# The last expert's second down group without split weights, other PSUM banks for some transposes, and a padded tile: a hybrid decoder trunk on one core

## The chip, the cores and the metric

One core of a Trainium2 chip runs the whole program in one launch. The metric is the device time of that launch in microseconds (us), lower is better. A measurement is the median over several runs; the profile is of one run more.

## The reference

Two layers on 512 tokens of width 1024, all in float32. Each layer is `h = LN(ALPHA*h + mixer(h))`, then `h = LN(ALPHA*h + FFN(h))`. The mixer is one projection `h @ w_in`, sparse attention and a short convolution, and an output projection by `w_o`. The FFN of layer 0 is a dense SwiGLU; that of layer 1, which ends the program, is a mixture of eight experts of hidden width 1408, of which each token takes two:

```python
for e in range(N_EXPERTS):
    out = out + gate[..., e:e + 1] * swiglu(h, wg[e], wu[e], wd[e])

def swiglu(h, wg, wu, wd):
    return (jax.nn.silu(h @ wg) * (h @ wu)) @ wd
```

The final layer norm follows, and its 512x1024 result is the output.

## The kernel before

**Products of split numbers.** A float32 operand is split into a high and a low part, and a product is three TensorE matmuls: high by high, low by high, high by low (`mm3`, L198). In the mixer and the dense FFN the parts are of type float32r (`split`, L141); in the expert stage they are float16. There `split16_ops` (L869) makes the high part on ScalarE (L873) and the low part on VectorE (L874), after a scaling by 256.

**The expert stage** (`moe`, L1005). The experts are sorted by load and taken in the order of `TURN`. Expert number e has a fixed room for tokens, `CAPS[e]`: 160, 168, 152, 144, 136, 132, 128, 128. The six with more than 128 rows deliver their result in two pieces of rows (`chunks`, L33). The hidden width is worked in two groups of 6 and 5 blocks of 128 (`groups`, L1010). For each expert and group the kernel streams pieces of the gate weight, the up weight and the down weight: `eblock` (L848) loads a piece by SyncE's queue into one of nine buffers, `split16` splits it, TensorE multiplies. `expert_gate` (L903) applies Silu; `expert_hidden` (L909) multiplies by the up product on VectorE (L913), then rounds to float16 on ScalarE (L914) and takes the rest on VectorE (L915), which gives the two parts `hh` and `hl`.

For the two experts with 128 rows the down product is by rows: the hidden parts are the stationary operand and the weights move through in two halves of 512 columns (`expert_down_rows`, L932, matmuls at L947). For the other six it is transposed, and `expert_out` (L979) turns it back: per piece of rows and half of the columns four TensorE transposes (L986) fill a PSUM bank, and ScalarE scales them out (L987). PSUM has eight banks by tag (L50): "mm" 2, "tr" 2, "s" 3, "po" 1. In `expert_out` the first half uses an "mm" bank and the second the only "po" bank, for both pieces. The code of `expert_out` is called behind the first piece of the next expert's first up product. The "s" banks hold the down product of an expert; they were emptied by `expert_end` (L967) just before.

**The end.** Once the last expert's gate product of group 0 is issued, GpSimd's queue fetches the sum over the other experts: 512 rows into `h` (L1064), and the rows that the last expert will change into `xl` (L1065). With the second group of the last expert all comes together. VectorE takes the statistics of the four tiles of `h` (`row_stats`, L993, and L1083); `roots` (L1021) gives one over the deviation (Sqrt on ScalarE, two small operations on VectorE); `rows_scaled` (L999) is two passes of 128x1024 per tile on VectorE, and `store` (L990) writes the tile by SyncE's queue. `last_rows` (L1040) adds a half of the last expert's product to `xl` (L1042) and takes its statistics (L1043). After both halves VectorE normalises `xl`, and GpSimd scatters its rows over the stored ones (L1114).

The order of instructions on each engine is laid down by a planner, which goes by program order among what is ready. `issue_after(x)` keeps VectorE's instructions of a block behind x. `self.low` is the latest split's VectorE instruction. So the statistics wait for the last up weight's split, and the scaling of the four tiles for the last down weight's split.

**The output projection of layer 1** (`out_proj`, L566). A pool holds the split pieces of W_o: seven of eight pairs of 128x1024 in it, the first in the common ring. In layer 1 three small tiles of the router lie ahead of them in the same pool (`route_sums`, L652): 512, 512 and 64 bytes per partition. In layer 0 nothing lies ahead of them.

Of the kernel before, what the change touches and what calls it, by code (L numbers as in the profile page):

```python
# [7 lines left out]
F32 = mybir.dt.float32  # L8
# [5 lines left out]
OP = mybir.AluOpType  # L14
# [3 lines left out]
S, D, NT, KD = 512, 1024, 4, 8  # L18
# [5 lines left out]
NE, FE, NFE = 8, 1408, 11  # L24
# [8 lines left out]
def chunks(e):  # L33

    c = CAPS[e]
    return [(0, c)] if c <= 128 else [(0, CH), (CH, c - CH)]


def by_rows(e):

    return CAPS[e] == 128


def packed(n, e):

    k = 512 // CAPS[e]
    return [(i, min(k, n - i)) for i in range(0, n, k)]
# [3 lines left out]
XS, WS, HS, GS = 2.0 ** 6, 2.0 ** 8, 2.0 ** 5, 2.0 ** 12  # L51
# [3 lines left out]
class Trunk:  # L55
# [596 lines left out]
    def route_sums(self, tp):  # L652


        nc = self.nc
        ones = tp.tile([128, 128], F32, name="ones32")
        nc.gpsimd.memset(ones, 1.0)
        x = tp.tile([128, 2, NE, KD], F32, name="gw")
        own = self.wr.rearrange("p k e -> p e k")
        for i in range(2):  # L660
            nc.vector.tensor_tensor(x[:, i], own, self.factors[:, i][:, None, :].to_broadcast([128, NE, KD]), op=OP.mult)
        nc.vector.tensor_copy(own, x[:, 0])
        s = tp.tile([128, 2, NE], F32, name="gs")
        nc.vector.tensor_reduce(s, x, axis=AX.X, op=OP.add)
        p = self.psum("po")
        nc.tensor.matmul(p[:, 0:2 * NE], ones, s.rearrange("p i e -> p (i e)"), start=True, stop=True)
        nc.vector.tensor_scalar(self.wsum[:, 0], p[:, 0:NE], -1.0, None, op0=OP.mult)
        nc.vector.tensor_copy(self.wsum[:, 1], p[:, NE:2 * NE])
# [234 lines left out]
    def expert_gate(self, parts):  # L903
# [2 lines left out]
            self.nc.scalar.activation(g[:, c], x, AF.Silu, scale=1.0 / (XS * WS))  # L906
        return g

    def expert_hidden(self, parts, g):  # L909
        nc = self.nc  # L910
        hh, hl = (self.mp.tile([128, 6 * CAP], F16, name=x, bufs=2) for x in ("ehh", "ehl"))
        for x, c in parts:
            nc.vector.scalar_tensor_tensor(g[:, c], x, HS / (XS * WS), g[:, c], op0=OP.mult, op1=OP.mult)  # L913
            nc.scalar.activation(hh[:, c], g[:, c], AF.Copy)  # L914
            nc.vector.tensor_tensor(hl[:, c], g[:, c], hh[:, c], op=OP.subtract)  # L915
        return hh, hl
# [12 lines left out]
                             lambda k: (hi[:, k - k0, c], lo[:, k - k0, c], hh[:, r(k)], hl[:, r(k)]), k0, k1,  # L929
                             first=f0 + k0 == 0 and m == 0, last=f0 + k1 == NFE and m == nm - 1, shared=True)  # L930

    def expert_down_rows(self, i0, e, f0, n, hh, hl, ys, finish=None):  # L932

        held = []
        for k0 in range(0, n, 2):
            k1 = min(n, k0 + 2)
            src = self.weights("moe_wd", i0, e, slice((f0 + k0) * 128, (f0 + k1) * 128), slice(0, D))
            hi, lo = self.split16(self.eblock([128, k1 - k0, D], src))
            held += [(k0 + k, hi[:, k], lo[:, k]) for k in range(k1 - k0)]
            if finish is not None and 0 < k0 and k1 < n:  # L940
                continue
            for half, y in enumerate(ys):
                c = slice(half * 512, half * 512 + 512)
                for k, h, l in held:
                    r = slice(k * 128, k * 128 + 128)
                    for a, b in ((hh, h), (hl, h), (hh, l)):
                        self.nc.tensor.matmul(y, a[:, r], b[:, c], start=f0 + k == 0 and a is hh and b is h,  # L947
                                              stop=f0 + k == NFE - 1 and b is l)
                if finish is not None and k1 == n:
                    finish(half)  # L950
            held = []

    def expert_rows(self, e, ys):

# [24 lines left out]
    def expert_out(self, e, yt):  # L979
        nc = self.nc  # L980
        for r, (s, n) in enumerate(chunks(e)):
            yr = self.mp.tile([128, D], F32, name="yr", bufs=2)[0:n]
            for half in range(2):
                p = self.psum("po" if half else "mm")
                for k in range(4):
                    nc.tensor.transpose(p[0:n, k * 128:(k + 1) * 128], yt[:, half * 4 + k, s:s + n], self.ident)  # L986
                nc.scalar.activation(yr[:, half * 512:half * 512 + 512], p[0:n], AF.Copy, scale=self.sgate[0:n, e, r:r + 1])  # L987
            self.add_rows(e, r, yr)
# [16 lines left out]
    def moe(self, l):  # L1005
        nc = self.nc
        mp = self.mp = self.pool("moe%d" % l)
        i0 = l // 2
        self.nblock = 0
        groups = [(0, 6), (6, 5)]  # L1010
# [10 lines left out]
        def roots(rs, mv):  # L1021
            nc.scalar.activation(rs, mv[:, :, 1:2], AF.Sqrt, bias=self.eps[0:rs.shape[0]], scale=ALPHA ** 2)
            nc.vector.reciprocal(rs, rs)
            nc.vector.tensor_scalar(rs, rs, ALPHA, None, op0=OP.mult)
# [8 lines left out]
        gb = end[:, 0:2]  # L1033
        self.ln_load(gb, self.t["ln2_g"][l], self.t["ln2_b"][l])
        final = TURN[-1]
        xl = end[:, 2]
        mv = mp.tile([128, NT, 2], F32, name="mv4")
        st2 = self.small.tile([128, 2, 6], F32, name="st")

        def last_rows(half, y):  # L1040
            c = slice(half * 512, half * 512 + 512)
            nc.vector.scalar_tensor_tensor(xl[:, c], y, self.sgate[:, final, 0:1], xl[:, c], op0=OP.mult, op1=OP.add)  # L1042
            nc.vector.bn_stats(st2[:, half], xl[:, c])  # L1043

        def ended(e, hid, ys):
            if by_rows(e):
                self.expert_down_rows(i0, e, *groups[1], *hid, ys)
                self.expert_rows(e, ys)
                return None
            self.expert_down(i0, e, *groups[1], *hid, ys)  # L1050
            return self.expert_end(e, ys)
        before = None
        for turn, e in enumerate(TURN):
            last = e == final
            after = None if last else TURN[turn + 1]
            xg = None if last else self.gather(after)
            up = lambda name, g, **kw: self.expert_up(i0, e, name, *groups[g], xs, **kw)

            gate = self.expert_gate(up("moe_wg", 0))
            yt = before and ended(*before)  # L1060
            if last:

                for tt in range(NT):
                    nc.gpsimd.dma_start(self.h[:, tt], self.abuf[tt * 128:(tt + 1) * 128])  # L1064
                nc.gpsimd.indirect_dma_start(out=xl, out_offset=None, in_=self.abuf[:, :],  # L1065
                                             in_offset=bass.IndirectOffsetOnAxis(ap=self.idx[:, e, 0:1], axis=0))
            out = (lambda: self.expert_out(before[0], yt)) if yt is not None else None
            hid = self.expert_hidden(up("moe_wu", 0, mid=out), gate)
            if turn + 2 < NE:
                self.slot_data(TURN[turn + 2])  # L1070
            gate = self.expert_gate(up("moe_wg", 1))
            ys = [self.psum("s") for _ in (range(2) if by_rows(e) else packed(KD, e))]
            (self.expert_down_rows if by_rows(e) else self.expert_down)(i0, e, *groups[0], *hid, ys)
            if turn == 0:
                self.slot_data(e)
            nxt = []
            mid = None if last else (lambda: nxt.extend(self.gather_t(after, xg)))
            hid = self.expert_hidden(up("moe_wu", 1, mid=mid), gate)
            before, xs = (e, hid, ys), nxt

        with self.tc.issue_after(self.low.ins):
            for tt in range(NT):
                nc.vector.bn_aggr(mv[:, tt], self.row_stats(self.h[:, tt]))  # L1083
            rs = self.small.tile([128, NT, 1], F32, name="rs4")
            roots(rs, mv)
            nc.vector.tensor_tensor(self.bad[:, 0:NT], mv[:, :, 1], mv[:, :, 1], op=OP.not_equal)

        def finish(half):
            if half == 0:
                with self.tc.issue_after(self.low.ins):  # L1090
                    for tt in range(NT):
                        self.rows_scaled(self.h[:, tt], mv[:, tt, 0:1], rs[:, tt], gb)
                        self.store(tt)
            last_rows(half, ys[half])
        self.expert_down_rows(i0, final, *groups[1], *hid, ys, finish)

        nl, nh, xl = 128, 1, end[:, 2:3]
        mv2 = mp.tile([nl, nh, 2], F32, name="mv2")
# [8 lines left out]
        p = self.psum("tr")  # L1107
# [3 lines left out]
        for r in range(nh):  # L1111
            self.rows_scaled(xl[:, r], mv2[:, r, 0:1], rs2[:, r], gb)
            i = self.dst[0:nl, final, r:r + 1]
# [121 lines left out]
```

## Time and profile before

| | |
|---|---|
| median of 3 runs (lowest to highest) | 1373.26 us (1372.77 to 1375.89) |
| the profiled run, its own time | 1373.08 us |
| span of its trace | 1371.2 us |
| mean granted TensorE clock | 0.994 of full speed |
| TensorE matmuls busy | 1329.4 us, 97% |
| VectorE busy | 867.5 us, 63% |
| ScalarE busy | 667.7 us, 49% |

The times in rows are microseconds from the start of the span. A matmul's duration is modelled from entering the array to leaving it, so neighbours overlap, and the pace of a row of matmuls is the distance of their starts. PEld is TensorE's load of the stationary operand. A busy share over the whole span says little here, since the engine that limits is another one at the end than before it; the views are read by stage.

### The profile page before, as it was taken

The page shows a single profiled execution, that of the slowest core. Times are in us where ns is not written, and L with a number is a line of the kernel's source. Part 1 is how long each engine was busy: PE and PEld are TensorE (multiplying, and loading weights), DVE is VectorE, ACT ScalarE, POOL GpSimd, SP SyncE. Part 2 cuts the span into 40 slices and gives each one's busy share as a digit, 9 for nine tenths or more (in the row PEclk, how much of TensorE's full clock was granted, in tenths as well). Part 3 has the DMA queues.
Part 4 walks back from the last instruction along what each step waited for, and adds up shares of the span by engine and source line. Part 5 has one row for each costly group of instructions (what it writes and reads, how often), then busy time and mean ns, then how long its engine had stood idle before and what let it go on. Part 6 is the DMA issues. An engine that isn't in the chain of part 4 may idle for free.

```text
span 1371.2 us, 26845 instructions
## 1 busy us (share of the span) xinstructions
PE 1329.4 (97%) x11478; PEld 1155.6 (84%) x11478; DVE 867.5 (63%) x1260; ACT 667.7 (49%) x948; POOL 72.4 (5%) x86
## 2 busy tenths in 40 slices
PE   5999999999999999999999999999999999999993
PEld 5888788898888888888887888889999999999872
DVE  7567665743333332228556665769688787788897
ACT  3575443323222322213565553427677677687881
POOL 3000000000000000000000000010011011010130
PEclk9999999999999999999999999999999999999997
DMA  8442020332323222322562020659899899899992
GB/s 254 128 123 62 32 62 33 122 102 83 123 66 118 92 95 104 109 92 60 158 165 63 31 63 1 218 218 364 299 350 355 275 345 372 308 353 370 384 377 103
DMA packets 137887, 241.10 MB, mean 176 GB/s; under 512 B 12891, under 2 KB 82619, under 8 KB 137765
## 3 DMA queue, kind: packets, MB, share of 16 engines
q1 hardware_dynamic: 132948, 223.20, 47.9%
q0 software_dynamic: 4816, 16.17, 4.1%
q8 instruction: 90, 1.47, 0.4%
q14 instruction: 33, 0.26, 0.1%
HBM read 227.75 MB, written 11.68 MB: 175 GB/s over the span
## 4 chain that ended last, share of the span: by engine, by line
PE 90%; DVE 6%; ACT 2%; issue 1%; DMA 1%; SPq 0%; POOL 0%; POOLq 0%; DVEq 0%; ACTq 0%
PE mm L205 47%; PE s L205 16%; PE tr L205 10%; PE po L491 3%; PE s L509 2%; PE s L475 2%; DVE wlo L874 1%; PE s L383 1%; PE po L205 1%; PE tr L475 1%; PE tr L509 1%; PE s L947 1%; DVE h L1002 1%; DVE h L1003 1%; PE tr L190 1%
## 5 line engine op out<-in xcount | busy, mean ns | idle before, releaser
L205 PEld LDWEIGHTS <-whi 128*128 128x128 f16 x3872 | 312.2, 98 | 1.3 <-issue 0.3
L147 ACT ACTIVATE whi<-stage 128x1024 fp32r<-128x1024 f32 x122 | 127.8, 1058 | 303.2 <-PE mm L205 187.5
L148 DVE TENSOR_TENSOR wlo<-stage,whi 128x1024 fp32r<-128x1024 f32 x118 | 143.7, 1223 | 195.1 <-ACT whi L147 192.7
L205 PE MATMUL mm<-xh,whi 128*128 128x512 f32 (+1 forms) x672 | 257.6, 384 | 0.3 <-DVE e L311 0.3
L205 PE MATMUL mm<-xh,wlo 128*128 128x512 f32 (+1 forms) x672 | 253.1, 377 | 0.4 <-DVE wlo L148 0.4
L205 PE MATMUL mm<-xl,whi 128*128 128x512 f32 (+1 forms) x672 | 252.4, 376 | 0.0
L874 DVE SCALAR_TENSOR_TENSOR wlo<-estage,whi 128x1536 f16<-128x1536 f32 (+4 forms) x106 | 201.6, 1918 | 37.3 <-ACT whi L873 37.2
L873 ACT ACTIVATE whi<-estage 128x1536 f16<-128x1536 f32 (+4 forms) x106 | 170.4, 1613 | 68.0 <-PE s L205 26.0
L205 PEld LDWEIGHTS <-wlo 128*128 128x128 f16 x1936 | 189.4, 98 | 0.0
L205 PEld LDWEIGHTS mm<-xh,wlo 128*128 128x128 f32 x672 | 127.0, 189 | 23.9 <-DVE wlo L148 0.6
L205 PEld LDWEIGHTS mm<-xh,whi 128*128 128x128 f32 x672 | 127.6, 190 | 21.6 <-issue 1.3
L205 PEld LDWEIGHTS mm<-xl,whi 128*128 128x128 f32 x672 | 127.4, 190 | 21.1
L205 PE MATMUL tr<-eh,whi 128*128 128x128 f16 (+6 forms) x704 | 133.8, 227 | 0.0
L205 PE MATMUL tr<-el,whi 128*128 128x128 f16 (+6 forms) x704 | 133.8, 227 | 0.0
L205 PE MATMUL tr<-eh,wlo 128*128 128x128 f16 (+6 forms) x704 | 133.8, 227 | 0.0
L205 PE MATMUL mm<-eh,whi 128*128 128x128 f16 (+6 forms) x704 | 132.3, 226 | 0.1
L205 PE MATMUL mm<-eh,wlo 128*128 128x128 f16 (+6 forms) x704 | 132.3, 226 | 0.0
L205 PE MATMUL mm<-el,whi 128*128 128x128 f16 (+6 forms) x704 | 132.3, 226 | 0.0
L874 DVE SCALAR_TENSOR_TENSOR wlo<-stage,whi 128x1536 f16<-128x1536 f32 (+5 forms) x56 | 102.5, 1839 | 23.7 <-ACT whi L873 22.5
L873 ACT ACTIVATE whi<-stage 128x1536 f16<-128x1536 f32 (+5 forms) x56 | 86.6, 1551 | 39.7 <-PE s L205 13.5
L205 PE MATMUL s<-ehh,whi 128*128 128x160 f16 (+5 forms) x528 | 102.6, 228 | 0.0
L205 PE MATMUL s<-ehh,wlo 128*128 128x160 f16 (+5 forms) x528 | 102.6, 228 | 0.0
(319 smaller groups left out, 2293.0 us busy)
## 6 DMA issues: line engine op xcount, KB each, us to landing
estage<-in_moe_wd_dram SPq DMA_DIRECT2D x29, 1024.0 KB
stage<-in_w_in_dram SPq DMA_DIRECT2D x32, 512.0 KB
estage<-in_moe_wu_dram SPq DMA_DIRECT2D x21, 768.0 KB
estage<-in_moe_wg_dram SPq DMA_DIRECT2D x18, 768.0 KB
stage<-in_ffn_wg_dram SPq DMA_DIRECT2D x11, 1024.0 KB
stage<-in_ffn_wu_dram SPq DMA_DIRECT2D x11, 1024.0 KB
stage<-in_ffn_wd_dram SPq DMA_DIRECT2D x11, 1024.0 KB
stage<-in_moe_wd_dram SPq DMA_DIRECT2D x11, 1024.0 KB
```

What stands on the lines that cost most here:

```text
L147: nc.scalar.activation(h, st, AF.Copy)
L148: (eng or nc.vector).tensor_tensor(o, st, h.bitcast(F32), op=OP.subtract)
L190: nc.tensor.transpose(p[:, k * 128:(k + 1) * 128], self.h[:, tt, kk * 128:(kk + 1) * 128], self.ident)
L205: self.nc.tensor.matmul(p, a, b, start=first and n == 0, stop=last and n == total - 1, skip_group_check=shared)
L383: nc.tensor.matmul(ph[r:r + 64, 0:256], e2[kv][:, c].rearrange("p g n -> p (g n)"), w1s[c // 8][:, c % 8], start=c < 2, stop=c > 13, skip_ ...
L475: nc.tensor.transpose(q[:, k * 128:k * 128 + 128], flat[:, c:c + 128], self.ident)
L491: nc.tensor.matmul(po[g * 64:g * 64 + 64, i * 128:i * 128 + 128], v[:, j, c:c + 64], flat[:, k:k + 128], start=False, stop=lbr == 1 and j ...
L509: nc.tensor.matmul(sp[:, wide[i]], qs[:, a, g, qi[i]], keys[:, br, g, 0:wide[i].stop - wide[i].start], start=keys is ks and i == blocks[0] ...
L873: nc.scalar.activation(hi[:, c], st[:, c], AF.Copy, scale=WS)
L874: self.low = nc.vector.scalar_tensor_tensor(lo[:, c], st[:, c], WS, hi[:, c], op0=OP.mult, op1=OP.subtract)
L947: self.nc.tensor.matmul(y, a[:, r], b[:, c], start=f0 + k == 0 and a is hh and b is h, stop=f0 + k == NFE - 1 and b is l)
L1002: self.nc.vector.scalar_tensor_tensor(x, x, mean, gb[0:m, 0], op0=OP.subtract, op1=OP.mult)
```

## The change

Three edits. In the last expert's second group the down weights are used in float32 as loaded, and the hidden values are one float32 tile, so that the three float16 matmuls become one float32 matmul; the order of VectorE's work around it is written anew. In `expert_out` the second piece of rows takes its banks from the tag "s". And the 64-byte tile beside W_o gets 256 bytes.

```diff
-        s = tp.tile([128, 2, NE], F32, name="gs")
+        s = tp.tile([128, 64], F32, name="gs")[:, 0:2 * NE].rearrange("p (i e) -> p i e", e=NE)
...
+    def expert_hidden_whole(self, parts, g):
+
+        for x, c in parts:
+            self.whole = self.nc.vector.scalar_tensor_tensor(g[:, c], x, HS / XS, g[:, c], op0=OP.mult, op1=OP.mult)
+        return g
...
+    def expert_down_whole(self, i0, e, f0, n, g, ys, finish):
+
+        w = []
+        for k0 in range(0, n, 2):
+            k1 = min(n, k0 + 2)
+            src = self.weights("moe_wd", i0, e, slice((f0 + k0) * 128, (f0 + k1) * 128), slice(0, D))
+            st = self.eblock([128, k1 - k0, D], src)
+            w += [st[:, k] for k in range(k1 - k0)]
+        for half, y in enumerate(ys):
+            c = slice(half * 512, half * 512 + 512)
+            for k in range(n):
+                self.nc.tensor.matmul(y, g[:, k * 128:k * 128 + 128], w[k][:, c], start=False, stop=k == n - 1)
+            finish(half)
...
-                p = self.psum("po" if half else "mm")
+                p = self.psum("s" if r else ("mm", "po")[half])
...
-            hid = self.expert_hidden(up("moe_wu", 1, mid=mid), gate)
+            hid = (self.expert_hidden_whole if last else self.expert_hidden)(up("moe_wu", 1, mid=mid), gate)
...
         with self.tc.issue_after(self.low.ins):
             for tt in range(NT):
                 nc.vector.bn_aggr(mv[:, tt], self.row_stats(self.h[:, tt]))
-            rs = self.small.tile([128, NT, 1], F32, name="rs4")
-            roots(rs, mv)
-            nc.vector.tensor_tensor(self.bad[:, 0:NT], mv[:, :, 1], mv[:, :, 1], op=OP.not_equal)
+        rs = self.small.tile([128, NT, 1], F32, name="rs4")
 
         def finish(half):
             if half == 0:
-                with self.tc.issue_after(self.low.ins):
+                stt = nc.vector.scalar_tensor_tensor
+                x = [self.h[:, tt] for tt in range(NT)]
+                with self.tc.issue_after(self.whole.ins):
+                    for tt in range(2):
+                        one = stt(x[tt], x[tt], mv[:, tt, 0:1], gb[:, 0], op0=OP.subtract, op1=OP.mult)
+                with self.tc.issue_after(one.ins):
+                    roots(rs, mv)
+                    nc.vector.tensor_tensor(self.bad[:, 0:NT], mv[:, :, 1], mv[:, :, 1], op=OP.not_equal)
                     for tt in range(NT):
-                        self.rows_scaled(self.h[:, tt], mv[:, tt, 0:1], rs[:, tt], gb)
+                        if tt >= 2:
+                            stt(x[tt], x[tt], mv[:, tt, 0:1], gb[:, 0], op0=OP.subtract, op1=OP.mult)
+                        stt(x[tt], x[tt], rs[:, tt], gb[:, 1], op0=OP.mult, op1=OP.add)
                         self.store(tt)
             last_rows(half, ys[half])
-        self.expert_down_rows(i0, final, *groups[1], *hid, ys, finish)
+        self.expert_down_whole(i0, final, *groups[1], hid, ys, finish)
```

`expert_down_rows` also loses its argument `finish` and the holding back of pieces that went with it; for the other expert with 128 rows it issues what it issued before.

## Rows read from the trace of the kernel before

**Rows 1.** Who waited for whom on TensorE, whole span: total us, times, longest

```profile
PE s L947 <- ACT ehh L914: 5.2, 1, 5.2
PE po L986 <- ACT yr L987: 1.9, 6, 0.3
```

**Rows 2.** Chain that ended last, 1300 us on: start us, us, what

```profile
1343.54 2.15 DVE wlo L874
...
1364.53 0.71 POOL out_dram L1114
```

**Rows 3.** Timeline, VectorE, 1340 to 1361 us: start us, us, engine line op out<-in xcount

```profile
1341.15 2.27 DVE L874 SCALAR_TENSOR_TENSOR wlo<-estage,whi 128x2048 f16<-128x2048 f32 x1
1343.34 0.20 DVE L1083 BATCH_NORM_AGGREGATE mv<-st 128x2 f32<-128x12 f32 x1
1343.46 2.23 DVE L874 SCALAR_TENSOR_TENSOR wlo<-estage,whi 128x2048 f16<-128x2048 f32 x1
1345.62 0.88 DVE L913 SCALAR_TENSOR_TENSOR eg<-tr,eg 128x512 f32<-128x512 f32 x2
1346.41 0.17 DVE L1023 RECIPROCAL rs<-rs 128x4 f32<-128x4 f32 x1
...
1346.55 1.22 DVE L874 SCALAR_TENSOR_TENSOR wlo<-estage,whi 128x1024 f16<-128x1024 f32 x1
1347.68 0.89 DVE L915 TENSOR_TENSOR ehl<-eg,ehh 128x512 f16<-128x512 f32 x2
1348.49 0.16 DVE L1024 TENSOR_SCALAR rs<-rs 128x4 f32<-128x4 f32 x1
1348.56 2.48 DVE L1002 SCALAR_TENSOR_TENSOR h<-h,mv,xl 128x1024 f32<-128x1024 f32 x2
...
1358.12 1.40 DVE L1042 SCALAR_TENSOR_TENSOR xl<-s,sgate,xl 128x512 f32<-128x512 f32 x2
...
1360.76 0.21 DVE L1099 BATCH_NORM_AGGREGATE mv<-st 128x2 f32<-128x12 f32 x1
```

**Rows 4.** Timeline, TensorE, the last up product and the last down product

```profile
1341.24 0.22 PE L205 MATMUL tr<-eh,wlo 128*128 128x128 f16 x1
...
1341.58 0.22 PE L205 MATMUL tr<-eh,wlo 128*128 128x128 f16 x1
1347.02 1.04 PE L947 MATMUL s<-whi,ehh 128*128 128x512 f16 x2 [5.22 <-ACT ehh L914]
...
1355.23 0.38 PE L947 MATMUL s<-wlo,ehh 128*128 128x512 f16 x1
```

**Rows 5.** Stretches: us, busy of PE, PEld, DVE, ACT, POOL, granted clock, DMA, GB/s

```profile
1275.00:1325.00 50.00, 50.00 (x703) 42.21 (x701) 47.46 (x36) 40.41 (x36) 3.82 (x2) 1.00 1.02 371
...
1347.00:1350.00 3.00, 2.61 (x6) 0.72 (x7) 3.00 (x6) 0.16 (x1) 0.00 (x0) 0.50 0.03 5
1350.00:1356.00 6.00, 5.61 (x25) 2.31 (x23) 6.00 (x6) 0.00 (x0) 0.00 (x0) 0.96 0.43 175
```

**Rows 6.** Chain through the first expert's gather, a float32 product, window 855 to 925 us

```profile
914.70 1.63 PE mm L723 x12
```

**Rows 7.** Loads of the stationary operand, by shape, whole span: busy us, mean ns

```profile
L723 PEld LDWEIGHTS mm<-xl,h 128*128 128x128 f32 x48 | 6.8, 190 | 0.3 <-DVE xl L716 0.2
```

**Rows 8.** Timeline, TensorE, the last of six waits in the transposes of second pieces

```profile
1270.15 0.22 PE L205 MATMUL tr<-eh,wlo 128*128 128x128 f16 x1
1270.70 0.63 PE L986 MATMUL po<-ident,yt 128*64 128x128 f32 x4 [0.34 <-ACT yr L987]
```

**Rows 9.** Chain, output projection of layer 0, then of layer 1

```profile
246.50 2.27 PE mm L205 x10
...
863.19 2.33 PE s L205 x10
...
870.10 2.29 PE mm L205 x10
```

**Rows 10.** Who waited for whom on SyncE's queue, 925 to 1335 us

```profile
SPq L855 <- DVE wlo L874: 281.4, 136, 7.2
```

More of the change, by code (lines that the diff above doesn't have):

```diff
@@ L930, in expert_down, with expert_down_rows @@
                              first=f0 + k0 == 0 and m == 0, last=f0 + k1 == NFE and m == nm - 1, shared=True)
-    def expert_down_rows(self, i0, e, f0, n, hh, hl, ys, finish=None):
-        held = []
+    def expert_down_rows(self, i0, e, f0, n, hh, hl, ys):
         for k0 in range(0, n, 2):
@@ L938, in expert_down_rows @@
             hi, lo = self.split16(self.eblock([128, k1 - k0, D], src))
-            held += [(k0 + k, hi[:, k], lo[:, k]) for k in range(k1 - k0)]
-            if finish is not None and 0 < k0 and k1 < n:
-                continue
             for half, y in enumerate(ys):
                 c = slice(half * 512, half * 512 + 512)
-                for k, h, l in held:
+                for k in range(k0, k1):
                     r = slice(k * 128, k * 128 + 128)
+                    h, l = hi[:, k - k0], lo[:, k - k0]
                     for a, b in ((hh, h), (hl, h), (hh, l)):
@@ L948, in expert_down_rows @@
                                               stop=f0 + k == NFE - 1 and b is l)
-                if finish is not None and k1 == n:
-                    finish(half)
-            held = []
+    def expert_down_whole(self, i0, e, f0, n, g, ys, finish):
[10 more added lines that the diff above has]
+            finish(half)
     def expert_rows(self, e, ys):
```

## The prediction

> **What bounds the kernel now.** I read the waits of TensorE first. Between the first layer norm and a flag after all work it has two of size [rows 1]: 5.2 us for the last expert's hidden values, and 1.9 us in six pieces in the transposes of `expert_out`. Its matmuls are busy throughout 1275 to 1325 us [rows 5]. So TensorE sets the time up to the last expert's second down group. I then followed the chain that ended last. Near the end it lies on VectorE, from the low parts at 1343.54 through scaling and `last_rows` to the scatter at 1364.53 [rows 2]. VectorE's timeline shows why [rows 3]: between the eighth statistics operation, which gives way to a low part at 1341.15, and the first pass of scaling at 1348.56 lie 7.41 us, mostly splits of the three down pieces. TensorE, done with the up product at 1341.80, stands still until 1347.02 [rows 4], then runs at half its clock until about 1350.5 (granted 0.50, which is 1.2 GHz, in that stretch [rows 5]), and yet starts its last matmul at 1355.23, before VectorE comes to `last_rows` at 1358.12. The end is VectorE's work in a row; TensorE hides in it.
>
> **Part 1, the last down group.** By the starts [rows 3], VectorE loses low parts of 2.19 (1341.15 to 1343.34), 2.16 (1343.46 to 1345.62) and 1.13 us (1346.55 to 1347.68), and the two L915 operations of 0.81 us (1347.68 to 1348.49): 6.29 us. The aggregate (0.12), the two gating operations (0.79) and the small ones (0.14 and 0.07) stay: 1.12 us. ScalarE loses three high parts and two roundings; with none of them on the chain once VectorE is free, I count nothing for them. The sort of wait that appears is VectorE on TensorE: the gating operation would be next at 1341.27, and the up product's first bank gets its last matmul six matmuls before the end, at 1341.24, out at 1341.46 [rows 4]. So the gating starts at about 1341.5, 0.25 us late, and ends at 1342.3; its second, short part finds its bank done at 1341.80. I add 0.1 us for the chain of small operations. Nothing else is queued behind this wait that could run before it, save two passes of scaling, 2.4 us, that the new order puts behind the gating. The Sqrt on ScalarE, its wait for the last aggregate included, lies beside these passes. The eight passes and `last_rows` are unchanged: from 1348.56 to 1360.76 is 12.2 us. VectorE gains 6.29 - 0.35 = 5.9 us, and the closing aggregate starts at 1354.9 instead of 1360.76.
>
> TensorE must keep up. A float32 matmul of this kernel is two instructions: the first expert's gather, a float32 product of 160 columns, issues 12 in 1.63 us, 0.136 us each [rows 6]. By columns that is 0.435 us for 512, an estimate from that row; ten matmuls are 20 instructions, 8.7 us, against 30 float16 ones before. They start at 1342.35, after 0.55 us of standing still in place of 5.2, and end at 1351.05. VectorE needs the second half's product at 1342.3 + 0.3 + 8 x 1.195 + 0.66 = 1352.8. TensorE has 1.8 us to spare, about what a spell at half clock as long as that of before (3.4 us, of which half would be lost) costs. So the float32 product costs nothing; without VectorE's passes as its cover it would cost its 8.7 us. The loads of the weights are SyncE's as before and their buffers have no later user in the expert stage. The stores of the four tiles move forward with the passes on the same queue, and nothing of SyncE or GpSimd is moved past them. The 10.4 us from the closing aggregate [rows 3] to the span's end, with the flag and the scatter [rows 2], stay as they are: the stores that the scatter follows are done earlier, not later.
>
> **Part 2, banks of the second pieces.** The second half of the second piece waits for ScalarE to empty the only "po" bank. In the last case the transposes start at 1270.70, the matmul ahead at 1270.15 [rows 8]: 0.55 us where its neighbours are 0.06 apart, so 0.49 us lost. The waits on TensorE are 0.3 us each because its modelled ends overlap [rows 1]. The other five are alike (starts 0.51 to 0.56 apart): in all 2.8 us. "s" banks are free there: the transposes read what the copies out of those banks have made, so they are empty by then, and the next expert's down product needs them a whole gate product later. What could be late next is the weights. ScalarE's four evictions of 0.67 us keep their sum, only the last comes up to 0.15 us earlier. SyncE's queue spends 281 of 410 us waiting for buffers, not the buffers for it [rows 10], and the view of TensorE's waits has none for a low part of this stage, so I let all of it through: 2.8 us, with bounds of 0 (some other engine paces) and 3.0. VectorE's unbroken work ahead of the gating begins behind a piece that waited for TensorE, so it moves forward whole.
>
> **Part 3, the padded tile.** Ten matmuls of the output projection take 2.27 us in layer 0, and 2.33 and 2.29 in layer 1, where the 64 bytes lie ahead [rows 9]. In layer 1, 4 x 2 x 7 x 3 = 168 matmuls read moved pieces. At 2 to 6 ns each that is 0.3 to 1.0 us if the address is the cause. The larger difference stands only where the splits run alongside, so I take 0.5 us, bounds -0.2 (other tiles of that pool move too) and 1.0. The small tile's own work is unchanged and lies beside the projection.
> The Trainium skill, SBUF — State Buffer, Operand start alignment, asks only for a multiple of the element's size, and says that this is about legality and not about speed. By it nothing follows from 64 bytes, and the sum would be 1364.4 instead of 1363.9; the rows differ by 1 to 3%, and no run here shows yet whether the address does it.
>
> **The sum** against the profiled run's own 1373.08 us (span 1371.2 and 1.9 around it; 0.2 below the median of 1373.26): -5.9 - 2.8 - 0.5 = 1363.9.
>
> **Rivals.**
> 1. *The banks' gain is given back.* The transposes come sooner, but the next pieces don't: ScalarE's evictions, or the transfers, pace the stage. For it: from 1275 to 1325 us the DMA share is 1.02, and VectorE is busy for 47.46 of 50 us [rows 5]. Against it: there too the loads wait for buffers [rows 10], and VectorE's idle pieces there end with ScalarE, which waited for TensorE. Only parts 1 and 3 are left: 1366.7.
> 2. *TensorE takes the place of VectorE.* The float32 product runs at 1.2 GHz throughout, as the float16 one did at first after standing still [rows 5]: 20 x 0.87 = 17.4 us, ends at 1359.75, and with one half of `last_rows` (0.66 + 0.60) the aggregate starts at 1361.0, 0.3 later than before. Only parts 2 and 3 are left: 1370.1. Against it: TensorE stands still 0.55 us, not 5.2, and at 1350 to 1356 the clock was back at 0.96 with matmuls in a row [rows 5].
> The Trainium skill, TensorE: Matmul & The Clock Gate, Part 1, calls the low clock the default that activity releases; both stretches fit that, and it would make a short stop cheap.
> 3. *Slower: the loads don't run beside the streams.* Each float32 instruction would wait for its own stationary operand, 0.19 us [rows 7], at half clock 0.38: 20 x 1.25 = 25.0 us, end at 1367.35, aggregate at 1368.6, 7.85 later than before; less 3.3 for the other parts: 1377.6. It decides from 1.02 us per instruction on, where the product would end past 1362.8. Against it: in the gather's row the starts are 0.136 us apart although a load takes 0.19 [rows 6, 7], so loads do run beside streams.
> 4. *The planner puts the gating ahead of the last statistics.* VectorE then idles for TensorE with work behind it: up to 1.2 us less gain, 1365.1. It belongs to the likeliest case's range.
>
> **How the numbers follow.** The forecast with all three parts, case 4 and the pad's bounds included, gets 0.66 (1362 to 1366); rival 1 0.20; rival 2 0.07; rival 3 0.03; 0.04 is left for no change that can be measured, if two parts fail. A measurement of this kernel can tell some 0.2%, 2.7 us, from no change, so faster starts below 1370.5. The first two cases, 0.86, and 0.05 of rival 2 are faster: 0.91. Same 0.05, slower 0.04. Single runs scatter by 3 us, and a spell of low clock of about 1.5 us can fall in or out. So the range is 1361.5 to 1368.2, which leaves out rivals 2 and 3 and the scatter of the first.
>
> **What would show it.** Right: L915 and L874 gone from VectorE behind the statistics, the gating at about 1338.5 (3 us earlier by parts 2 and 3), the first scaling pass right behind it, 20 float32 instructions 0.43 us apart, done before the eighth pass, and `last_rows` without a wait. TensorE has no wait for L987. Rows of ten matmuls of W_o in layer 1 take 2.27 us. Wrong: VectorE waiting for TensorE ahead of L1042; a granted clock of 0.5 there; new waits of TensorE for low parts; L205 in layer 1 still at 2.29 to 2.33.

## The result, and the profile after

The changed kernel takes 1366.34 us (median of 6 runs, 1363.85 to 1368.1); the kernel before, beside it, 1375.04 us (6 runs, 1372.77 to 1376.8). The ratio is 0.9935, interval 0.9919 to 0.9951: some 9 us faster, 0.65%. The profiled run took 1367.07 us, with a span of 1365.3 us and a mean granted clock of 0.995.

The tail first. VectorE's timeline of the kernel after, from the last low part of the up weights on (columns as in [rows 3]: start, us, engine, line, operation, and in brackets the idle time before it and its releaser):

```profile
1333.38 1.48 DVE L874 SCALAR_TENSOR_TENSOR wlo<-stage,whi 128x1280 f16<-128x1280 f32 x1
1334.78 1.87 DVE L1010 BATCH_NORM_STATS2 st<-h 128x6 f32<-128x512 f32 x3
...
1337.89 0.69 DVE L1010 BATCH_NORM_STATS2 st<-h 128x6 f32<-128x512 f32 x1 [0.58 <-DMA h<-abuf]
...
1339.78 0.69 DVE L1010 BATCH_NORM_STATS2 st<-h 128x6 f32<-128x512 f32 x1 [0.53 <-DMA h<-abuf]
...
1341.18 0.21 DVE L1097 BATCH_NORM_AGGREGATE mv<-st 128x2 f32<-128x12 f32 x1
1341.30 0.83 DVE L912 SCALAR_TENSOR_TENSOR eg<-tr,eg 128x512 f32<-128x512 f32 x2
1342.05 2.47 DVE L1106 SCALAR_TENSOR_TENSOR h<-h,mv,xl 128x1024 f32<-128x1024 f32 x2
...
1347.04 4.87 DVE L1113 SCALAR_TENSOR_TENSOR h<-h,rs,xl 128x1024 f32<-128x1024 f32 x4
1351.82 1.40 DVE L1056 SCALAR_TENSOR_TENSOR xl<-s,sgate,xl 128x512 f32<-128x512 f32 x2
...
1354.45 0.21 DVE L1120 BATCH_NORM_AGGREGATE mv<-st 128x2 f32<-128x12 f32 x1
```

Against [rows 3], the low parts and the two subtractions between statistics and scaling are gone. The gating (L912) comes right behind the last aggregate, scaling right behind the gating, and `last_rows` (L1056) has no wait in brackets. What is new are two waits, 0.58 and 0.53 us, of the statistics for rows of `h` that GpSimd's queue fetches. From the last low part to the closing aggregate it is now 1354.45 - 1333.38 = 21.07 us; before it was 1360.76 - 1334.78 = 25.98. TensorE in the same stretch, which answers to [rows 4] (columns as above):

```profile
1342.00 8.85 PE L964 MATMUL s<-estage,eg 128*128 128x512 f32 x20 [1.60 <-DVE eg L912]
1356.43 0.16 PE L1129 MATMUL tr<-badb,ones 128*1 128x1 bf16 x1 [5.58 <-DVE badb L1127]
```

The twenty float32 instructions take 8.85 us, ending at 1350.85, one microsecond before `last_rows` starts. TensorE stood still for 1.60 us in place of 5.22. The stretches of the kernel after (columns as in [rows 5]) show the clock:

```profile
968.00:972.00 4.00, 4.00 (x38) 3.25 (x38) 3.06 (x4) 1.86 (x4) 1.13 (x2) 1.00 0.75 218
...
1080.00:1085.00 5.00, 5.00 (x36) 4.53 (x36) 2.77 (x4) 0.95 (x3) 1.92 (x2) 0.66 0.84 275
...
1342.00:1346.00 4.00, 4.00 (x10) 1.85 (x11) 4.00 (x8) 0.00 (x0) 0.00 (x0) 1.00 0.00 0
1346.00:1351.00 5.00, 4.85 (x12) 1.86 (x10) 5.00 (x5) 0.00 (x0) 0.00 (x0) 1.00 0.36 148
```

The float32 product has the full clock throughout, where [rows 5] had 0.50. But a stretch at 1080 us, which had the full clock before, now has 0.66 in the mean. The stretch at 968 us was the other way round, as these rows of the kernel before show (same columns):

```profile
968.00:972.00 4.00, 4.00 (x31) 3.58 (x31) 2.27 (x4) 0.89 (x2) 1.88 (x2) 0.57 0.77 268
...
1080.00:1085.00 5.00, 5.00 (x49) 4.15 (x49) 3.09 (x4) 2.00 (x4) 1.92 (x2) 1.00 0.76 218
```

The banks. TensorE's timeline of the kernel after at the place of [rows 8]:

```profile
1266.62 0.22 PE L205 MATMUL tr<-eh,wlo 128*128 128x128 f16 x1
1266.68 0.60 PE L1000 MATMUL mm<-ident,yt 128*80 128x128 f32 x4
1267.12 0.60 PE L1000 MATMUL po<-ident,yt 128*80 128x128 f32 x4
1267.55 0.71 PE L1000 MATMUL s<-ident,yt 128*64 128x128 f32 x5
```

The second piece goes into "s" banks without a gap. The view of TensorE's waits no longer has the second line of [rows 1].

A ledger of the two profiled runs, by the starts of the same TensorE work in both timelines:

| work that starts | before, us | after, us | after - before |
|---|---|---|---|
| first transposes of the program | 11.32 | 12.16 | +0.84 |
| gather 1 (gathers counted from 0 in the order taken) | 965.57 | 966.97 | +1.40 |
| first `expert_out` | 994.15 | 994.12 | -0.03 |
| gather 3 | 1079.09 | 1078.04 | -1.05 |
| third `expert_out` | 1107.14 | 1107.74 | +0.60 |
| sixth `expert_out` | 1267.55 | 1266.68 | -0.87 |
| gather 7 | 1292.84 | 1291.44 | -1.40 |
| closing aggregate (VectorE) | 1360.76 | 1354.45 | -6.31 |

Six steps hold one `expert_out` with two pieces each: they give 0.56, 0.46, 0.52, 0.46, 0.49 and 0.53, 3.02 us. The step at gather 1 gives 1.43, since the spell of low clock at 968 us is not there; the step at gather 3 costs 1.65, with the spell at 1080 us. The 1.40 us ahead of gather 1 lie in work that the change doesn't touch, but for the pad; 0.84 of them are there when the first transposes start. The tail gives 4.91. Sum: 1.40 - 1.43 + 1.65 - 3.02 - 4.91 = -6.31. From the closing aggregate to the span's end it takes 10.84 us in place of 10.41, so the spans differ by 5.9.

### The profile page after: what moved, and what is told of

Same layout as the page of the kernel before. It is cut to its first block, busy times and chain, and to the rows that moved or that the text cites. A ratio compares the mean times of both kernels' runs of the same rounds, so it can differ in the third digit from the quotient of the medians.

```text
span 1365.3 us, 26812 instructions
## 1 busy us (share of the span) xinstructions
PE 1329.0 (97%) x11468; PEld 1156.3 (85%) x11468; DVE 861.4 (63%) x1255; ACT 661.3 (48%) x943; POOL 70.1 (5%) x86
## 4 chain that ended last, share of the span: by engine, by line
PE 90%; DVE 4%; DMA 3%; ACT 1%; issue 1%; SPq 0%; POOL 0%; POOLq 0%; DVEq 0%; ACTq 0%
PE mm L205 46%; PE s L205 15%; PE tr L205 11%; PE po L491 3%; PE s L509 2%; PE s L475 2%; PE s L383 1%; PE po L205 1%; PE tr L475 1%; PE tr L509 1%; PE s L950 1%; DMA h<-abuf 1%; DMA abuf<-yr,dst 1%; PE tr L190 1%; PE po L485 1%; PE mm L843 1%
## 5 line engine op out<-in xcount | busy, mean ns | idle before, releaser
L874 DVE SCALAR_TENSOR_TENSOR wlo<-estage,whi 128x1536 f16<-128x1536 f32 (+4 forms) x103 | 195.9, 1918 | 37.0 <-ACT whi L873 36.9
L873 ACT ACTIVATE whi<-estage 128x1536 f16<-128x1536 f32 (+4 forms) x103 | 165.6, 1612 | 66.1 <-PE s L205 26.0
```

The source lines that it names most:

```text
L873: nc.scalar.activation(hi[:, c], st[:, c], AF.Copy, scale=WS)
L874: self.low = nc.vector.scalar_tensor_tensor(lo[:, c], st[:, c], WS, hi[:, c], op0=OP.mult, op1=OP.subtract)
```

## The experiments

**The float32 group alone.** The kernel before with the third and largest edit of the diff, without the banks and without the pad.

> The kernel before with the float32 down group and its new order alone (banks and tile as before). My theory, VectorE's work in a row sets the end: low parts and L915 gone, 5.9 us less than before, ratio 0.9957. In the profile TensorE keeps its six waits in the transposes of second pieces. If the fetch of the 512 rows of h is what holds the statistics in the changed kernel because TensorE got ahead of the transfers by the banks, then here, 2.8 us later, VectorE waits for no fetch and the stretch from the last low part of the up weights to the closing aggregate is 6 us shorter than before. Rival, the fetch's landing is late in any case by the luck of the transfers: the same 0.5 us waits for the fetch stand here too and the gain is about 5 us (0.9964).

Measured: 1368.32 us (7 runs) against 1373.71 (24 runs), ratio 0.9957 (0.9941 to 0.9973): 5.9 us by the ratio, 5.4 between the medians. Its view of TensorE's waits keeps the line of `expert_out` (columns: total us, times, longest):

```profile
PE po L1000 <- ACT yr L1001: 1.9, 6, 0.3
...
PE s L964 <- DVE eg L912: 0.7, 1, 0.7
```

From the last low part to the closing aggregate its VectorE timeline has 1354.02 - 1333.80 = 20.22 us, with a wait of 0.35 for fetched rows: 5.76 less than before, 6.11 without that wait. So part 1 has its 5.9 us, and the wait for `h` comes without the banks too.

**The banks alone.** One line:

```diff
-                p = self.psum("po" if half else "mm")
+                p = self.psum("s" if r else ("mm", "po")[half])
```

> The kernel before with the banks of the second pieces alone. Theory: six waits of 0.49 us go, 2.8 us less than before, ratio 0.998; no wait of TensorE for L987 in the profile, each next expert's transposes 0.5 us earlier than before relative to the one ahead. Rival 1, the stage is paced by something else or the gain is lost at the end, where VectorE then waits for the fetched rows: 0 to 1.7 us less, 0.9990 to 1.0.

Measured: 1373.19 us (12 runs), ratio 0.9992 (0.9979 to 1.0004): nothing that can be told. Yet the six waits are gone in its trace and each step is 0.5 us shorter. What took their place is in its stretches (columns as in [rows 5]):

```profile
968.00:972.00 4.00, 4.00 (x28) 3.45 (x28) 3.06 (x4) 1.27 (x3) 1.72 (x2) 0.72 0.74 222
...
1080.00:1085.00 5.00, 5.00 (x32) 4.15 (x33) 3.09 (x4) 2.01 (x4) 1.92 (x2) 0.74 0.75 212
```

Two spells of low clock, behind gathers 1 and 3, where the profile of before has one. By the starts of the same work in both timelines the six steps give 3.0 us, and the step at gather 3 takes 1.64 back. The tail takes 26.63 us in place of 25.98, 0.55 of it a wait for fetched rows. So the time lies where the rival had it, but the rival's reason, the end, is the smaller part. All runs together have a lower clock too: 0.9902 over 12 runs against 0.9925 over 24 runs before. That mean doesn't price the spells, since it also counts low clock in the tail, where VectorE sets the time, and after TensorE's work.

**The pad alone.** One line:

```diff
-        s = tp.tile([128, 2, NE], F32, name="gs")
+        s = tp.tile([128, 64], F32, name="gs")[:, 0:2 * NE].rearrange("p (i e) -> p i e", e=NE)
```

> The kernel before with the padded tile alone. Theory: 168 matmuls of the output projection of layer 1 at 2.27 us per ten in place of 2.29 to 2.33, 0.5 us less than before, which the time of the launch can hardly show (ratio 0.9996), but the starts in the profile do: 25 matmuls in 5.67 us in place of 5.83. Rival, the pace isn't the address's: the starts stay 0.229 to 0.233 us apart. Second rival, the pace gets better and ScalarE, still busy with the first gate weight's split as it arrives, makes the transposes of the logits wait: the projection is not shorter in all.

Measured: 1374.68 us (12 runs), ratio 1.0007 (0.9996 to 1.0018). The chain through its output projection of layer 1 (start, us, what), which answers to the second and third of [rows 9]:

```profile
863.44 2.27 PE s L205 x10
...
870.25 2.27 PE mm L205 x10
```

These rows of ten take the 2.27 us of layer 0, in place of 2.33 and 2.29; the float32 group without the pad has 2.33 and 2.29 at the same places. The pad changes nothing but where the tiles behind it lie, so the address does set the pace of these rows. The Trainium skill, SBUF — State Buffer, Operand start alignment, says of its rule that it is about legality, not speed, and that nothing was timed for it; a price of the address, such as these rows show, isn't in it. But from the product with the small tile ahead of the projection to the first expert's gather it takes 53.19 us with the pad and 53.20 without. Up to the transposes behind the projection 0.2 us are gained (14.57 against 14.78), and then lost again. ScalarE's timeline of the padded kernel there (columns as in VectorE's):

```profile
872.34 1.58 ACT L873 ACTIVATE whi<-stage 128x768 f16<-128x768 f32 x2 [3.47 <-DMA stage<-in_moe_wg_dram]
873.83 1.06 ACT L685 ACTIVATE xh<-tr 128x512 f32<-128x512 f32 x2
```

The operations that the logits wait for (L685) stand behind two splits of gate weights, and those wait for a transfer. When it lands sets this stretch, and not when the projection ends. That is the second rival, with a transfer behind ScalarE's delay.

**The changed kernel again**, to see what of its profile stays the same.

> The changed kernel itself, on the chip of the three runs with one part each. Theory, the parts add up: -5.9 - 2.8 - 0.3 = -9 us against the kernel before, 0.9935. If the banks' gain is partly lost at the end to the fetched rows, the whole is less than the sum of the parts by about 1 us, and VectorE waits about 1 us for the fetch ahead of the statistics of the third and fourth tile here and not with the float32 group alone.

Measured: 1366.79 us (6 runs), ratio 0.9947 (0.9929 to 0.9965), which holds the 0.9935 that was forecast. VectorE's timeline:

```profile
1332.55 1.48 DVE L874 SCALAR_TENSOR_TENSOR wlo<-stage,whi 128x1280 f16<-128x1280 f32 x1
...
1339.26 0.89 DVE L912 SCALAR_TENSOR_TENSOR eg<-tr,eg 128x512 f32<-128x512 f32 x2
...
1352.47 0.21 DVE L1120 BATCH_NORM_AGGREGATE mv<-st 128x2 f32<-128x12 f32 x1
```

19.92 us from low part to closing aggregate, no wait for fetched rows: 6.06 less than before, where 5.9 were forecast. The spell of low clock at 1080 us is there again.

**The gather by pieces.** What stands just ahead of the spells of low clock is a gather. Its transposes (`gather_t`) alternate between the two pieces of rows. This experiment lets the piece be the outer loop; the transposes are the same, in another order:

```diff
-            for k in range(n if xs is not None else 0):
-                c = slice((k0 + k) * 128, (k0 + k) * 128 + 128)
-                for h, (s, m) in enumerate(chunks(e)):
+            for h, (s, m) in enumerate(chunks(e)):
+                for k in range(n if xs is not None else 0):
+                    c = slice((k0 + k) * 128, (k0 + k) * 128 + 128)
```

> The changed kernel with one edit more: in the gathered rows' transposes (L843) the loop over the two pieces of rows goes outside the loop over columns, so that 80-row and 52-, 56- or 64-row transposes no longer alternate. In the traces so far the gathers with a second piece of 52, 56 and 64 rows issue a transpose every 0.2 us, those with 72, 88 or 48 more rows (one piece of 128) every 0.08 to 0.11, and the granted clock falls to 0.5 for 3 us right behind one or two of the slow ones. Theory, the alternation of a piece over 64 rows with one of at most 64 is what costs: three gathers take 1.3 us in place of 3.4, 6 us less than the changed kernel, and with no sparse stretch the clock stays at 1.00 there, another 1 to 3 us; 1358 to 1361 us, ratio about 0.989 to the kernel before. Rival, the row count alone costs (a load of 52 rows is slow): nothing changes, 0.9945.

Measured, on top of the changed kernel: **1359.2 us** (4 runs, 1358.75 to 1360.74), ratio 0.989 (0.9876 to 0.9905), faster than both kernels. Gather 1 in TensorE's timeline, first of the kernel after, then of this one:

```profile
966.97 1.25 PE L843 MATMUL mm<-ident,x 80*128 80x80 f32 x6
968.15 1.31 PE L843 MATMUL po<-ident,x 80*128 80x80 f32 x6
969.39 0.90 PE L843 MATMUL mm<-ident,x 80*128 80x80 f32 x4
```

```profile
966.23 0.69 PE L843 MATMUL mm<-ident,x 80*128 80x80 f32 x6
966.86 0.74 PE L843 MATMUL po<-ident,x 80*128 80x80 f32 x6
967.53 0.61 PE L843 MATMUL mm<-ident,x 80*128 80x80 f32 x4
```

Sixteen transposes take 1.9 us in place of 3.3. The stretches of this run (columns as in [rows 5]) have the full clock at both places:

```profile
968.00:972.00 4.00, 4.00 (x59) 3.94 (x59) 2.94 (x4) 1.58 (x4) 2.98 (x2) 1.00 0.80 254
...
1080.00:1084.00 4.00, 4.00 (x61) 4.00 (x59) 1.97 (x3) 2.19 (x2) 1.07 (x2) 1.00 0.88 271
```

The mean clock of its runs is 0.9965. Its statistics waited 1.39 us for fetched rows in the profiled run, so the tail of this profile is not the shortest that this kernel can have.

**The same edit on the kernel before**, alone and with the banks, to price the banks where gathers are quick.

> The kernel before with the gather's transposes by piece alone: the base for the run with the banks. Theory: 6 us less and a mean clock of 0.994 or more in all runs, ratio 0.994 to 0.995. Rival (row count): 1.0.

> The kernel before with the gather's transposes by piece and the banks of the second pieces. The banks alone gave 0.9992 where 0.998 was forecast; in their trace the six waits are gone (0.5 us each) and the clock falls behind two gathers, with a mean clock of 0.990 against 0.9925 in the runs of the kernel before. Theory, the gain was there and the low clock behind the slow gathers took most of it: with the slow gathers gone the banks give 2.8 us against the run with the gather's edit alone. Rival, the banks' gain is lost at the end (the fetched rows): less than 1.5 us apart here too.

Measured: 1367.96 us (5 runs), ratio 0.9955 (0.9943 to 0.9968), for the gather alone; 1365.19 (6 runs), ratio 0.9936 (0.9924 to 0.9948), with the banks. The difference is 2.77 us, give or take 1, the banks' 2.8, at nearly the same clock (0.9936 and 0.9932); by the starts in the two timelines the six steps give 3.02. The gather's edit alone gives 6.2 us, as forecast; its clock, forecast at 0.994 or more in all runs, is 0.993 in three of five. Three gathers of 1.4 us are 4.2 of the 6.2. About as much comes out if the time missing to full clock, span times (1 - clock), is taken off the spans, 1361.7 and 1357.4. The rest is missing time that went.

**Ten products more** in the changed kernel's tail, to measure how much TensorE has to spare. Between the halves stand ten further float32 matmuls into a bank that nobody reads:

```diff
+            if half:
+                t = self.psum("tr")
+                for j in range(10):
+                    k = j % n
+                    self.nc.tensor.matmul(t, g[:, k * 128:k * 128 + 128], w[k][:, c], start=j == 0, stop=j == 9)
```

> The changed kernel with ten float32 matmuls more, into a bank that nothing reads, between the first and the second half of the last down product: 20 instructions, 8.6 us of TensorE. Theory, TensorE has 1.6 us to spare below VectorE's passes: the product of the second half is done 7.0 us after VectorE is ready for it and the closing aggregate comes 7.0 us later than in the changed kernel, relative to the start of the first gating operation (13.15 us there). Rival, TensorE already sets the end: 8.6 us later. Second rival, at 1.2 GHz for part of it: over 8.6.

Measured: one run, 1373.06 us. Its TensorE timeline, then its VectorE timeline:

```profile
1345.43 8.75 PE L967 MATMUL tr<-estage,eg 128*128 128x512 f32 x20
1354.01 4.45 PE L969 MATMUL s<-estage,eg 128*128 128x512 f32 x10
```

```profile
1358.51 0.75 DVE L1061 SCALAR_TENSOR_TENSOR xl<-s,sgate,xl 128x512 f32<-128x512 f32 x1 [6.17 <-PE s L969]
...
1360.02 0.21 DVE L1125 BATCH_NORM_AGGREGATE mv<-st 128x2 f32<-128x12 f32 x1
```

From the gating (1340.34) to the closing aggregate it is 19.68 us, against 13.15 in the kernel after: 6.5 more, where 7.0 were forecast, for 8.6 more on TensorE. So about 2.1 us were spare. One statistics operation of 0.6 us runs during the wait here, in another order than in the kernel after; without it 1.5 us are left.

**The old order with the new product.** The changed kernel, with the roots and all eight passes given to the planner behind the last low part again:

```diff
-                with self.tc.issue_after(self.whole.ins):
-                    for tt in range(2):
-                        one = stt(x[tt], x[tt], mv[:, tt, 0:1], gb[:, 0], op0=OP.subtract, op1=OP.mult)
-                with self.tc.issue_after(one.ins):
-                    roots(rs, mv)
...
+                with self.tc.issue_after(self.low.ins):
                     for tt in range(NT):
...
+                        self.rows_scaled(self.h[:, tt], mv[:, tt, 0:1], rs[:, tt], gb)
                         self.store(tt)
```

> The changed kernel with its third edit of the last expert undone: the float32 product stays, but the four closing statistics, the square roots and all eight scaling passes are again given to the planner behind the last low part, as before, so that three scaling passes (each about 1.2 us) come ahead of the two gating operations, and the float32 product starts some 3.6 us later. Theory (the gating has to come first because TensorE has only some 1.6 us to spare behind VectorE's passes): last_rows waits for the product's second half, and from the last low part of the up weights to the closing aggregate it takes 2.0 us more than the 19.9 us of the changed kernel without a wait for fetched rows (bounds 0.5 and 2.3); some 1368.5 us, ratio to the kernel before 0.9953. Rival (the order is worth nothing, the gain is all in the splits that went): the same 19.9 to 20.3 us and 1366.5 us, no wait of last_rows for TensorE.

Measured: 1370.3 us (7 runs), ratio 0.9968 (0.9955 to 0.9981). TensorE's timeline, VectorE's timeline, and the stretches (columns as in [rows 5]):

```profile
1344.62 10.47 PE L964 MATMUL s<-estage,eg 128*128 128x512 f32 x20 [3.83 <-DVE eg L912]
```

```profile
1333.78 1.48 DVE L874 SCALAR_TENSOR_TENSOR wlo<-stage,whi 128x1280 f16<-128x1280 f32 x1
...
1355.13 0.75 DVE L1056 SCALAR_TENSOR_TENSOR xl<-s,sgate,xl 128x512 f32<-128x512 f32 x1 [2.73 <-PE s L964]
...
1356.64 0.21 DVE L1113 BATCH_NORM_AGGREGATE mv<-st 128x2 f32<-128x12 f32 x1
```

```profile
1344.60:1346.00 1.40, 1.38 (x2) 0.84 (x3) 1.40 (x4) 0.00 (x0) 0.00 (x0) 0.50 0.06 12
1346.00:1348.00 2.00, 2.00 (x3) 0.67 (x2) 1.97 (x4) 0.00 (x0) 0.00 (x0) 0.52 0.00 0
1348.00:1350.00 2.00, 2.00 (x6) 0.95 (x5) 2.00 (x3) 0.00 (x0) 0.00 (x0) 1.00 0.85 344
```

From low part to closing aggregate 22.86 us, 2.94 more than the 19.92 of the changed kernel's second profile. To put the gating first is worth that much, and more than my bound of 2.3, for a second reason: after standing still for 3.83 us TensorE starts at half its clock, and the product takes 10.47 us in place of 8.85. The start comes 1344.62 - 1333.78 = 10.84 us after the low part, against 7.46 there (1340.01 by its TensorE timeline). 3.38 later and 1.62 longer, less about 2.0 to spare, is 3.0.

This order follows the rule of before, but it is not the order of before: there the scaling waited for the last down split, so the gating came ahead of it [rows 3]; with the down splits gone nothing holds the scaling back. Of the 6.06 us in the tail, 25.98 - 22.86 = 3.12 come without the new order, the other 2.94 with it.

## Why the prediction was right, and where it was not

The forecast was 1363.9 us, 9.2 below its profiled run; measured are 1366.34 and 8.7 below the kernel before beside it. The likeliest case came, with its three sizes not all as I had them. That the two agree to half a microsecond is in part luck: the two profiled runs are 6.0 us apart (1373.08 and 1367.07), the repeat gives 7.3 by its ratio, part 3 gave nothing, and two things that the sum doesn't have, spells of low clock and a wait for fetched rows, differ from run to run by 1 to 2 us each.

**Part 1 was right, mechanism and size.** Alone it gives 5.9 us by the ratio, and 6.06 in the tail of the profile without waits for `h`. The 20 float32 instructions took 8.85 us, their starts 0.43 apart, as estimated from the gather of 160 columns. Rival 3, weight loads not beside streams, is excluded by that pace. Rival 2 is half right: with the old order TensorE stood still for 3.83 us and then had a clock of 0.50. With the new order the stop was 1.60 us (0.45 in the repeat) and the clock 1.00, and that is why the rival did not come. The Trainium skill, TensorE: Matmul & The Clock Gate, Part 1, which calls the low clock the default that activity releases, agrees with both.

**The gating came in the order forecast, and later.** It stands behind the last aggregate, so rival 4 did not happen. The wait of 0.25 us for TensorE did not come: the gating starts 0.12 us after the aggregate does, since the statistics themselves came later than the up product. In the repeat, without a wait for fetched rows, it starts 6.71 us behind the last low part, where 6.72 were forecast. In the profile after it came at 1341.30 and not at 1338.5: 1.40 us of that lie ahead of gather 1, 1.11 are the waits for fetched rows, 0.22 the two spells of low clock (1.65 less 1.43). TensorE's slack, which I put at 1.8 us, measures 1.5 to 2.1 by the ten products more.

**Missing from the sum: the wait for fetched rows.** "VectorE's unbroken work ahead of the gating begins behind a piece that waited for TensorE, so it moves forward whole" took for granted that `h` is there whenever VectorE comes. The wait is 1.11 us in the profile after, 0 in that of the same kernel again, 0.35 with part 1 alone, 1.39 with the quicker gather, and 0.62 with the pad alone, which has neither the banks nor the float32 group. The larger part of that last one stands in this line of its VectorE timeline:

```profile
1338.36 0.69 DVE L996 BATCH_NORM_STATS2 st<-h 128x6 f32<-128x512 f32 x1 [0.52 <-DMA h<-abuf]
```

So these profiles don't show that the change makes the wait longer; when the fetch lands differs from run to run. "The 10.4 us from the closing aggregate" stayed no more exactly: they are 10.84 in the profile after, but 10.86 too in the kernel before with the quicker gather.

**Part 2 was right in size, and incomplete.** The six steps give 3.02 us in the trace, and 2.77 us between two kernels with quick gathers. Rival 1 (the pieces pace the stage) is excluded by both. But with the old gather the banks alone come out at 0.9992, 1.1 us and inside the scatter. In their profile a second spell of low clock takes 1.64 of the 3.0 us that they give, and a wait for fetched rows 0.55. My step "I let all of it through" looked only at engines and transfers that could be late next. Spells of low clock stood in the range as scatter "of about 1.5 us"; that the change itself might make one regular I did not see. Each of the five profiles of kernels with the banks and the old gather (after, its repeat, the banks alone, ten products more, the old order) has a spell at gather 3, none of the three without the banks (before, the float32 group alone, the pad alone). Eight profiles don't prove it, since spells come and go in the kernel before too, and why the banks should bring it on is open. In the whole change the loss is small in the mean of the runs: span times (1 - clock), which can be compared where the tail is the same, is 7.7 us there, 8.4 in its repeat and 7.6 in the float32 group alone.

**Part 3 was mis-sized: 0.5 forecast, nothing found** (1.0007, 0.9996 to 1.0018). The first link holds, 2.33 to 2.27 us per ten matmuls. The failed step is "168 matmuls at 2 to 6 ns each": the gain stood ahead of the first of the logits' transposes, some 3 ns each and 0.2 us in all, with less than 1 ns each behind them, and the work there is released by a transfer and by ScalarE, which I had not looked at.

The parts alone add up to less than the whole: by the ratios -5.9, -1.1 and +1.0 make -6.0, the whole gives -8.9 in one comparison and -7.3 in another (0.9947). The intervals of the parts are 3 to 4 us wide, so no further effect can be told from this.

## What to carry to other kernels

Where VectorE paces a short stage with the splitting of weights and TensorE stands still, one float32 matmul in place of three of low precision buys VectorE's time with TensorE's; put the operation that starts TensorE first, for the work behind it hides the product, and the stop stays short (here stops of up to 1.60 us kept the full clock, 3.83 and 5.22 us lost it). When a wait goes, look behind it not only for the next engine but for spells of low clock near slow stretches of TensorE, and price the change also with those stretches mended. A row that quickens locally pays only if the next thing behind it was waiting for that row.

## What the runs showed of the hardware that was not expected

- **Alternating transposes of large and small pieces are slow.** In the gathers of 80 rows and 52, 56 or 64 rows TensorE issues 16 transposes in 3.3 us, 0.2 us each; grouped by piece they take 1.9 us. By the single starts in that trace a transpose takes 0.15 to 0.16 us where the piece changes and 0.06 to 0.13 inside a piece, so the cost stands at the change. Gathers whose pieces both have more than 64 rows (80 with 88 or 72) don't show it in the old order: 0.07 to 0.08 each. The Trainium skill, TensorEngine Tiling (Array Packing), Key Properties, says that a change of tiling mode drains TensorE. If pieces of up to 64 rows use another mode than larger ones, the runs fit this rule; that they do is not in the trace.
- **The clock falls where the trace shows no idle time of TensorE.** In the stretches with 0.57 to 0.74 its matmuls count as busy for the whole of the time (their durations are modelled, so a short stop inside would not show); what stands ahead are those slow gathers. With quick gathers the spells at 968 and 1080 us are gone. A slow gather is not enough, though: gather 5, of the kernel after in these lines of TensorE's timeline, is as slow, and no profile has a spell behind it.

```profile
1188.24 1.28 PE L843 MATMUL mm<-ident,x 80*128 80x80 f32 x6
1189.46 1.33 PE L843 MATMUL po<-ident,x 80*128 80x80 f32 x6
1190.72 0.91 PE L843 MATMUL mm<-ident,x 80*128 80x80 f32 x4
```

- **64 bytes ahead of them, in place of 256, slow the matmuls that read the 128x512 float32r pieces of W_o**, by 1 to 3% (2.29 and 2.33 us per ten against 2.27).
